# Sums inside DRAM placed over heads 0 to 3 instead of in one block, four of them listed for the page stage; sample values, index scales and index keys reordered

## The chip, the cores and the metric

The kernel runs on one core of a Trainium2 chip. Its engines are the matrix engine (PE, whose weight loads are shown as PEld), the vector engine (DVE), the scalar engine (ACT), GpSimd (POOL) and the sync engine (SP), which here only issues DMAs; POOL issues some too. Each engine works through its own queue of instructions in the order in which the program gives them, and waits on semaphores. The metric is the device time of one execution in microseconds (us), lower is better; the number given is the median of several executions.

## The reference

One inference step of a single decoder layer with two groups of heads: sparse indexer attention (8 heads of 128) and gated linear attention (4 heads, keys of 128, values of 256). There are 512 prompt tokens and 64 sample tokens (8 sequences of 8), which attend to 1024 cached positions held in pages of 128. Everything is float32, the model width is 2048.

```python
h = RMSNorm(x)                                  # prompt and sample rows alike
z = einsum('btd,de->bte', h, w_in)              # one projection for all groups
qa, ka, va, ga, qi, ki, wi, qb, kb, vb, gb, ab = split(z)
# sparse attention: score every position by the indexer, keep the best 256 (128 in the prompt), attend to those
dots = einsum('bthd,bsd->btsh', qi, ki) * D_IDX ** -0.5
sc   = einsum('btsh,bth->bts', relu(dots), wi)  # causal, then top_k
p    = softmax(q . k_selected * DH_A ** -0.5);  o = p . v_selected
# gated linear attention: S <- diag(a_t) S + k_t v_t ; o_t = q_t S  (chunked)
y = RMSNorm(x + concat(silu(ga) * o_A, silu(gb) * o_B) @ w_out)
```

It returns y, the new keys, values and index keys, and the new recurrent states.

## The kernel before

**Weights.** Each 128x512 block of weights comes through `wload`: a DMA from SP into `w_raw` (three buffers), a cast on ACT to the rounded half `w_hi` (L196, five buffers), and the rest `w_lo = w_raw - w_hi` (L199, five buffers), which POOL makes in heads 0 to 3 and DVE elsewhere (`lo_eng`). PE multiplies xh by w_hi, xl by w_hi and xh by w_lo (L251 in columns of 288, L256, and L664 to L666 in columns of 512), so each product has nearly float32's precision. `wloads` and `rounded` hold the DMAs and casts so far, and `issue_after` puts an instruction behind one of them.

**Heads.** `head(h)` projects q, k, v and g for one attention head, scores it (L736 to L738, `pq` from `kh`, `kl` and `qh`, `ql`; `kh` is the cast of the rotated keys, L632), and writes the gated result to DRAM. Head 0 is followed by `vgroup(0)`, which makes the values of heads 0 to 3. Into the heads a background is woven: first the indexer's scores for the sample pages (`sample_scores`, index keys `kc` from pages, split into `kch` and `kcl`, L505 to L517), then the top-k rounds (MAX8 and MATCH_REPLACE on DVE), and from head 4 on the *page stage*, `units`: it loads pages of cached keys and values (`kt`, `vt`) and scores them (`pS`, L283 to L286), one beat of a generator for each weight block.

**Sums of output weights.** The output projection uses sums of blocks of `w_out`. `block_parts` yields 16 parts of 512 KB into the DRAM tensor `spill_t[1]` (`st` in the profile): each is a copy from DRAM to DRAM, issued by SP, and then an accumulating DMA issued by POOL. Parts 0 to 7 add further blocks of `w_out`; parts 8 to 11 add the finished parts 0 to 3, and parts 12 to 15 the finished parts 8 to 11. Other sums (`spill_t[0]`) are made by `block_sums` in the page stage, eight of them. Before, the list `started` issues one copy with each weight load after `vgroup(0)` (16 in a row, L194), and the list `added` one add behind each of POOL's w_lo from head 2 on (16 in a row, L203).

**Scales.** `squares` and what follows make `rstd`, the norm's factor for each token, by matmuls with diagonal matrices (`ps_st`, L405). It scales the index keys (`kiT`, `ab`, L409 to L414) and twice the index weights of the sample (`wiT`, called `sS` in the profile, L416), which a matmul `pU` (L418) spreads.

**Recurrence.** `recur` runs a head of gated linear attention over four prompt blocks: state update `pUg`, output `pO` (L1232), state `Sst` (L1241), then the sample part, which needs the sample's values `vs` as halves (`vSg` loaded from DRAM, cast at L1220, subtracted at L1221).

**What sets the order.** The program is written in Python order, but a scheduler with a timeline of its own orders the instructions of each engine; `high_priority` and `issue_after` steer it. So the order built can differ from the text.

Of the kernel before, what the change touches and what calls it, by code (L numbers as in the profile page):

```python
# [20 lines left out]
P = 128  # L21
# [98 lines left out]
def build(tc, I, O):  # L120
# [61 lines left out]
        return t[:, 32:544] if far else t[:, :512]  # L182

    SUMS = ((0, 0), (0, 1), (1, 1), (1, 0))
    started, added = [], []

    def wload(src, far=0):
        with tc.high_priority(offset=WOFF):
            raw = wp.tile([P, 512], F32, name="w_raw", tag="w_raw", bufs=3)
            d = sy.dma_start(raw, src)  # L190
            wloads.append(d.ins if hasattr(d, "ins") else d)
            if started:
                with tc.issue_after(wloads[-1]):
                    sy.dma_start(*started.pop(0))  # L194
            hi = wp.tile([P, 512], F32R, name="w_hi", tag="w_hi", bufs=5)
            c = se.copy(hi, raw)  # L196
            rounded.append(getattr(c, "ins", c))
            lo = low_tile(wp, 5, far)
            c = lo_eng[0].tensor_tensor(out=lo, in0=raw, in1=hi.bitcast(F32), op=ALU.subtract)  # L199
            if lo_eng[0] is po_:  # L200
                if added:
                    with tc.issue_after(getattr(c, "ins", c)):
                        po_.dma_start(*added.pop(0), accum_op=ALU.add)  # L203
        return hi, lo

    first_w = {}
# [188 lines left out]
    def token_scales():  # L395
        se.activation(sst, sst, AF.Sqrt, bias=eps, scale=1.0 / D)
        ve.reciprocal(out=sst, in_=sst)
        ve.tensor_tensor(out=sst2, in0=sst, in1=sst, op=ALU.mult)
        for j in range(2):
            pst = mm1("ps_st")  # L400
            for i in (range(4), (4,))[j]:
                n = (P, TS)[j]
                dg = pr.tile([P, P], F32, name="dg", bufs=2)
                ve.tensor_scalar(out=dg[:, :n], in0=ident[:, P - n :], scalar1=sst[:, i : i + 1], scalar2=None, op0=ALU.mult)
                pe.matmul(pst[:, P * (i % 4) : P * (i % 4) + n], ones, dg[:, :n], start=True, stop=True)  # L405
            c = (slice(0, TP), slice(TP, T))[j]
            se.copy(rstd[:, c], pst[:, : c.stop - c.start])

        ve.tensor_mul(kiT, kiT, rstd[0:64])  # L409
        sy.dma_start(O["kiT"], kiT)  # L410
        ab = keys[:, :T]
        ve.tensor_tensor(out=v2(ab[64:96]), in0=ps0[64:96], in1=v2(rstd[64:96]), op=ALU.mult)
        se.copy(abS[64:96], ab[64:96])
        ve.tensor_tensor(out=abS[96:128], in0=ab[64:96], in1=abS[64:96].bitcast(F32), op=ALU.subtract)  # L414
        for _ in range(2):
            ve.tensor_tensor(out=wiT[:, TP:T], in0=wiT[:, TP:T], in1=rstd[0:16, TP:T], op=ALU.mult)  # L416
        pu = mm1("pU")
        pe.matmul(pu[:, :TS], e16[0:16], wiT[:, TP:T], start=True, stop=True)  # L418
        for half in range(2):
            for e in range(2):  # L420
                c = 16 * half + DT * e
                ve.tensor_tensor(
                    out=wall[:, half].rearrange("p (m e) c -> p m e c", e=2)[:, :, e, c : c + DT],
                    in0=pu[:, :TS].rearrange("p (m e t) -> p m e t", e=2, t=DT)[:, :, e, :],
                    in1=dt8.unsqueeze(1).to_broadcast([P, 4, DT]), op=ALU.mult,
                )
# [52 lines left out]
    def sample_scores():  # L479
# [14 lines left out]
        for half in range(2):  # L494
            for grp in range(2):
                for m in range(4):
                    if half and m == grp == 0:
                        weigh(0)
                    b = 2 * m + grp
                    hr, other = ((slice(0, 64), slice(64, 128)), (slice(64, 128), slice(0, 64)))[m % 2]  # L500
                    if m % 2 == 0:
                        kc = pa.tile([P, 512], F32, name="kc", bufs=2)
                    raw = kc[hr]
                    page_dma(lambda j: raw[:, P * j : P * (j + 1)], lambda r: I["cidx"][r].rearrange("o d s -> (o d) s"), b * NPAGE + 4 * half, 4)
                    kch = pa.tile([P, 512], F32R, name="kch", tag="kch", bufs=2)  # L505
                    se.copy(kch[hr], raw)
                    po_.tensor_copy(kch[other], raw)
                    kcl = pa.tile([P, 512], F32R, name="kcl", bufs=2)
                    with tc.high_priority(offset=WOFF // 2):
                        ve.tensor_tensor(out=kcl[hr], in0=raw, in1=kch[hr].bitcast(F32), op=ALU.subtract)  # L510
                        se.copy(kcl[other], kcl[hr].bitcast(F32))
                    yield
                    pq = mm1("pq")
                    pe.matmul(pq, lq[b], kch, start=True, stop=False)
                    pe.matmul(pq, lq[b], kcl, start=False, stop=True)
                    rl = pa.tile([P, 512], F32, name="rl", bufs=8)
                    se.activation(rl, pq, AF.Relu)  # L517
                    rls.append(rl)
# [132 lines left out]
    def vgroup(g, step):  # L651
# [46 lines left out]
            if g < 2:  # L698
                sy.dma_start(O["v"][r, cols], vt)
        if g == 0:  # L700
            po_.memset(vaS[:TS], 0.0)
        to = vaS[TS:, cols] if g < 2 else ev.tile([P, 512], F32, name="v_smp", tag="e1", bufs=2)[TS:]
        se.copy(to, accs[4][:TS])
        ve.tensor_tensor(out=to, in0=accs[4][TS:], in1=to, op=ALU.add)
# [77 lines left out]
    def head(h, bg, n):  # L782
        if h == 1:
            q, k = qk1
        else:
            q = head_q(h)
            pump(bg, n)
            k = head_k(h)
            pump(bg, n)
        if h == 0:  # L790
            for f in (head_q, head_k):
                qk1.append(f(1))
                pump(bg, n)
            vgroup(0, lambda k: pump(bg, 2) if k % 4 == 3 else None)
            filler[0] = None
            for _ in first:
                pass
            pa_s.close()
            px["p"], px["s"] = pool("pd1", 1)
            pump(bg, 3)  # L800
            for to, src, _ in block_parts():
                started.append((to, src))
        if h == 2:
            assert not started
            for to, _, more in block_parts():
                added.append((to, more))
        Pi = head_scores(h, q, k)
        if h == 4:
            vgroup(1, lambda k: None)
        v = head_v(h)  # L810
        g1 = head_g(h)
        pump(bg, min(n, 4))
        head_out(h, Pi, v, g1)

    qk1 = []


    mixS = gaS
# [1 line left out]
    def units(un, hg, pages):  # L820
        later, count = [], [0, 0]

        def block_sums():
            n = count[1]
            count[1] += 1
            t = un.tile([P, 4, 512], F32, name="bs", tag="kv", bufs=pages)
            for j, (half, q) in enumerate(SUMS):
                sy.dma_start(t[:, j, :], I["wo"][q, :, 8 * half + n, :])

            def add():  # L830
                ve.tensor_tensor(out=t[:, 0:2, :], in0=t[:, 0:2, :], in1=t[:, 1:3, :], op=ALU.add)
                ve.tensor_tensor(out=t[:, 2, :], in0=t[:, 2, :], in1=t[:, 0, :], op=ALU.add)
                ve.tensor_tensor(out=t[:, 3, :], in0=t[:, 3, :], in1=t[:, 2, :], op=ALU.add)

            later.append((count[0] + 2, add))
            later.append((count[0] + 3, lambda: sy.dma_start(spill_t[0][:, :, n, :], t)))

# [22 lines left out]

        for _ in unit_steps(un, hg, fetch, rest):
            count[0] += 1
            while later and later[0][0] <= count[0]:
                later.pop(0)[1]()
            yield
        for _, f in later:
            f()
# [1 line left out]
    def unit_steps(un, hg, fetch, rest):  # L869
        kv = fetch(0, 0, 0)  # L870
        yield
        if hg == 0:
            yield from rest(2)
        for w in range(2):
            qz = ev.tile([P, 4, 4, 32], F32, name="qz", tag="e0", bufs=2)
            po_.memset(qz, 0.0)
# [100 lines left out]
    head(2, bg, 4)  # L977
    head(3, bg, 4)
    lo_eng[0] = ve
    assert not added  # L980
    with tc.issue_after(px["end"]):
        for _ in bg:
            pass
# [225 lines left out]
    def recur(h, eL, qE, kDt, ks):  # L1209
        vtok = gl.tile([P, 4, DV], F32, name="vtok")  # L1210
        sv = spill_v[2 + h // 2][:, DV * (h % 2) : DV * (h % 2) + DV]
        with tc.issue_after(wloads[-1]):
            sy.dma_start(vS[:TS], sv[TP:])
            sy.dma_start(vtok, sv[:TP].rearrange("(i p) c -> p i c", p=P))
        vs = [gl.tile([96, DV], F32R, name=f"vs{w}") for w in range(2)]
        for w in range(2):
            r = slice(32 * w, 32 * w + 32)
            with tc.issue_after(rounded[-1]):
                for r0 in (0, 32):
                    se.copy(vs[w][r0 : r0 + 32], vS[r])  # L1220
            ve.tensor_tensor(out=vs[w][64:96], in0=vS[r], in1=vs[w][r].bitcast(F32), op=ALU.subtract)  # L1221


        osb = gl.tile([P, 5, DV], F32, name="osb")
        ss = gl.tile([P, 5], F32, name="ss", bufs=2)
        S = None
        for i in range(4):
# [11 lines left out]
            with ahead():  # L1239
                if S is None:  # L1240
                    ve.tensor_copy(Sn, pU[:, :DV])  # L1241
                else:
                    ve.scalar_tensor_tensor(out=Sn, in0=S, scalar=eL[:, i : i + 1], in1=pU[:, :DV], op0=ALU.mult, op1=ALU.add)
            S = Sn
        sy.dma_start(O["sp"][h], S)

        pO = mm1("pO")
# [425 lines left out]
```

## Time and profile before

| | us |
|---|---|
| median of 3 executions | 1194.14 (1193.59 to 1195.24) |
| the profiled execution | 1196.54 |
| its span in the trace | 1194.8 |
| PE busy | 1180.8 |
| DVE / ACT / POOL busy | 727.3 / 585.2 / 311.7 |
| DMA moved | 259.98 MB, mean 218 GB/s |

The profiled execution lies 2.40 us above the median, and 1.74 us of its time lie outside the span. PE is the engine to watch: the others have idle time everywhere. PE's matmuls overlap, so a busy time per matmul can't be added up; waits of PE are where time can be won. Below, start times are counted from the start of the span, DMA times go from issue to landing, and a wait is put down to what ended it.

### The profile page before, as it was taken

To read this page: it belongs to the slowest core of one execution; us is meant where nothing else is said; L and a number is where in the kernel's file an instruction comes from. 1 tells how busy PE (TensorE), PEld (TensorE's weight loads), DVE (VectorE), ACT (ScalarE), POOL (GpSimd) and SP (SyncE) were. 2 spreads that over 40 slices of the span, in tenths; PEclk is the share of its full clock that TensorE was granted. 3 is DMA by queue.
4 is the path that set the end of the run, shared out by engine and by line. 5 is a ranking of instruction groups with operands and counts; after the bars stand their busy time and mean duration, and the time that the engine had idled before them with its cause. 6 is when DMAs were issued, how large, how long until landed. Compare 5 with 4: busy or idle time off the path is not lost.

```text
span 1194.8 us, 22991 instructions
## 1 busy us (share of the span) xinstructions
PE 1180.8 (99%) x8389; PEld 1040.1 (87%) x8389; DVE 727.3 (61%) x1347; ACT 585.2 (49%) x1045; POOL 311.7 (26%) x495
## 2 busy tenths in 40 slices
PE   9999999999999999999999999999999999999997
PEld 8999987899989778899988769778899999888886
DVE  7678899799646433575445424434556444657786
ACT  6887564444443232354344435336367533544454
POOL 1225665536621110200213311321042211012100
PEclk9999999999999999999999999999999999999999
DMA  8552233777973999998857675667715377669873
GB/s 298 204 171 102 91 106 108 267 242 165 223 179 91 365 315 359 339 321 307 287 198 267 221 258 204 220 226 246 258 50 178 123 253 233 228 169 238 249 229 119
DMA packets 142419, 259.98 MB, mean 218 GB/s; under 512 B 15633, under 2 KB 38818, under 8 KB 141730
## 3 DMA queue, kind: packets, MB, share of 16 engines
q1 hardware_dynamic: 136370, 243.83, 60.7%
q0 software_dynamic: 4928, 13.11, 6.4%
q10 hardware_dynamic: 1008, 1.57, 0.4%
q8 instruction: 66, 1.08, 0.4%
q14 instruction: 47, 0.39, 0.1%
HBM read 224.62 MB, written 50.48 MB: 230 GB/s over the span
## 4 chain that ended last, share of the span: by engine, by line
PE 90%; DMA 4%; DVE 3%; issue 1%; SPq 1%; ACT 1%; POOL 0%; DVEq 0%; ACTq 0%; POOLq 0%
PE ps_g L251 37%; PE ps_g L256 6%; PE ps_g L664 5%; PE ps_g L666 5%; PE ps_g L665 5%; PE acc L1392 4%; PE acc L1393 4%; PE acc L1394 4%; DMA w_raw<-in_w 2%; PE pS L286 2%; PE pOs L286 2%; PE acc_s L1398 1%; PE acc_s L1397 1%; PE ps_v L660 1%; PE ps_v L661 1%
## 5 line engine op out<-in xcount | busy, mean ns | idle before, releaser
L251 PE MATMUL ps_g<-xh,w_hi 128*128 128x288 f32 x1312 | 391.6, 298 | 0.0
L251 PE MATMUL ps_g<-xl,w_hi 128*128 128x288 f32 x1312 | 287.9, 297 | 0.0
L251 PE MATMUL ps_g<-xh,w_lo 128*128 128x288 f32 x1312 | 283.9, 295 | 0.4 <-DVE w_lo L219 0.2
L196 ACT CAST w_hi<-w_raw 128x512 fp32r<-128x512 f32 x252 | 154.0, 619 | 261.8 <-PE ps_g L251 82.5
L251 PEld LDWEIGHTS ps_g<-xh,w_hi 128*128 128x128 f32 x1312 | 246.3, 188 | 3.6 <-issue 1.7
L199 DVE TENSOR_TENSOR w_lo<-w_raw,w_hi 128x512 fp32r<-128x512 f32 x188 | 132.6, 712 | 183.5 <-ACT w_hi L196 174.9
L251 PEld LDWEIGHTS ps_g<-xl,w_hi 128*128 128x128 f32 x1312 | 212.1, 188 | 2.3 <-issue 1.2
L251 PEld LDWEIGHTS ps_g<-xh,w_lo 128*128 128x128 f32 x1312 | 211.2, 188 | 1.8 <-DVE w_lo L219 0.5
L199 POOL TENSOR_TENSOR w_lo<-w_raw,w_hi 128x512 fp32r<-128x512 f32 x64 | 87.6, 1370 | 55.2 <-ACT w_hi L196 46.8
L664 PE MATMUL ps_g<-w_hi,xh 128*128 128x512 f32 x256 | 100.9, 396 | 0.0
L666 PE MATMUL ps_g<-w_hi,xl 128*128 128x512 f32 x256 | 100.3, 392 | 0.0
L665 PE MATMUL ps_g<-w_lo,xh 128*128 128x512 f32 x256 | 100.1, 391 | 0.0
L1387 DVE TENSOR_TENSOR w_lo<-w_raw,w_hi 128x1024 fp32r<-128x1024 f32 (+1 forms) x60 | 68.4, 1150 | 40.1 <-ACT w_hi L1385 39.7
L1385 ACT CAST w_hi<-w_raw 128x1024 fp32r<-128x1024 f32 (+1 forms) x60 | 59.6, 994 | 64.6 <-PE acc_s L1397 27.2
L1393 PE MATMUL acc<-w_lo,fh 128*128 128x512 f32 x216 | 84.0, 389 | 0.0
L1394 PE MATMUL acc<-w_hi,fl 128*128 128x512 f32 x216 | 84.0, 389 | 0.0
L1392 PE MATMUL acc<-w_hi,fh 128*128 128x512 f32 x216 | 83.5, 389 | 0.0
L666 PEld LDWEIGHTS ps_g<-w_hi,xl 128*128 128x128 f32 x256 | 48.1, 188 | 10.7 <-issue 0.8
L664 PEld LDWEIGHTS ps_g<-w_hi,xh 128*128 128x128 f32 x256 | 48.0, 188 | 10.0 <-DVE ev_t L624 0.3
L665 PEld LDWEIGHTS ps_g<-w_lo,xh 128*128 128x128 f32 x256 | 48.1, 188 | 9.7
L1394 PEld LDWEIGHTS acc<-w_hi,fl 128*128 128x128 f32 x216 | 40.5, 188 | 8.5
L1392 PEld LDWEIGHTS acc<-w_hi,fh 128*128 128x128 f32 x216 | 40.6, 188 | 8.4
(396 smaller groups left out, 2085.2 us busy)
## 6 DMA issues: line engine op xcount, KB each, us to landing
w_raw<-in_w SPq DMA_DIRECT2D x188, 256.0 KB, 4.0
kt<-in_ck SPq DMA_DIRECT2D x128, 256.0 KB, 5.1
vt<-in_cv SPq DMA_DIRECT2D x128, 256.0 KB, 5.3
w_raw<-in_wv SPq DMA_DIRECT2D x64, 256.0 KB, 3.4
w_raw<-st SPq DMA_DIRECT2D x32, 512.0 KB, 4.8
w_raw<-in_wo SPq DMA_DIRECT2D x20, 512.0 KB, 5.5
st<-in_wo SPq DMA_DIRECT2D x16, 512.0 KB, 4.9
bs<-in_wo SPq DMA_DIRECT2D x32, 256.0 KB, 5.4
```

The lines of the kernel that those rows point to most:

```text
L196: c = se.copy(hi, raw)
L199: c = lo_eng[0].tensor_tensor(out=lo, in0=raw, in1=hi.bitcast(F32), op=ALU.subtract)
L251: pe.matmul(ps[:, j, :HT], wt, xt[k][:, j * HT : (j + 1) * HT], start=(k == 0 and n in (0, 2)), stop=(k == NK - 1 and n > 3))
L256: m = pe.matmul(ps[:, 0, :TQ], wt[:, c], xt[:, P:T], start=(k == 0 and n == 0), stop=(k == NK - 1 and n == 2))
L664: pe.matmul(accs[i], xh[k][:, c], wh, start=a, stop=False)
L665: pe.matmul(accs[i], xh[k][:, c], wl, start=False, stop=False)
L666: m = pe.matmul(accs[i], xl[k][:, c], wh, start=False, stop=b)
L1385: se.copy(hi, raw)
L1387: ve.tensor_tensor(out=lo, in0=raw, in1=hi.bitcast(F32), op=ALU.subtract)
L1392: pe.matmul(acc, f[0][:, k, c], wh, start=a, stop=False)
L1393: pe.matmul(acc, f[0][:, k, c], wl, start=False, stop=False)
L1394: return pe.matmul(acc, f[1][:, k, c], wh, start=False, stop=b)
```

## The change

1. Copies and adds of the DRAM sums go by a table, `moves`: after `vgroup(0)` the weight loads are counted in slots; the copy of part n goes with slot 2n and its add with slot 2n + 6, for parts 0 to 11. Parts 12 to 15 go to a list `late`, out of which `block_sums` takes them in the page stage.
2. The two products of the sample's index weights with `rstd` stand ahead of those of the index keys.
3. The index key pages `kc` have three buffers instead of two.
4. The page stage rests three beats instead of two at its start; its list `later` may hold entries out of order.
5. The memset of `vaS` on POOL is put behind the last w_lo.
6. In `recur` the split of the sample's values stands behind the second block instead of ahead of the first.

```diff
+    moves, slot = ({}, {}), [None]
+
+    def move(side, lead):
+        for f in moves[side].pop(slot[0], ()):
+            with tc.issue_after(lead):
+                f()
...
             wloads.append(d.ins if hasattr(d, "ins") else d)
-            if started:
-                with tc.issue_after(wloads[-1]):
-                    sy.dma_start(*started.pop(0))
+            move(0, wloads[-1])
...
-            if lo_eng[0] is po_:
-                if added:
-                    with tc.issue_after(getattr(c, "ins", c)):
-                        po_.dma_start(*added.pop(0), accum_op=ALU.add)
+            lows.append(getattr(c, "ins", c))
+            move(1, lows[-1])
+            if slot[0] is not None:
+                slot[0] += 1
...
+        for _ in range(2):
+            ve.tensor_tensor(out=wiT[:, TP:T], in0=wiT[:, TP:T], in1=rstd[0:16, TP:T], op=ALU.mult)
         ve.tensor_mul(kiT, kiT, rstd[0:64])
...
-        for _ in range(2):
-            ve.tensor_tensor(out=wiT[:, TP:T], in0=wiT[:, TP:T], in1=rstd[0:16, TP:T], op=ALU.mult)
...
-                        kc = pa.tile([P, 512], F32, name="kc", bufs=2)
+                        kc = pa.tile([P, 512], F32, name="kc", bufs=3)
...
-            po_.memset(vaS[:TS], 0.0)
+            with tc.issue_after(lows[-1]):
+                po_.memset(vaS[:TS], 0.0)
...
-            for to, src, _ in block_parts():
-                started.append((to, src))
-        if h == 2:
-            assert not started
-            for to, _, more in block_parts():
-                added.append((to, more))
+            parts = list(block_parts())
+            for n, (to, src, more) in enumerate(parts[:12]):
+                moves[0][2 * n] = [partial(sy.dma_start, to, src)]
+                moves[1][2 * n + 6] = [partial(po_.dma_start, to, more, accum_op=ALU.add)]
+            late.extend(parts[12:])
+            slot[0] = 0
...
+            if n >= 4:
+                to, src, more = late.pop(0)
+                later.append((count[0] + 1, lambda: sy.dma_start(to, src)))
+                later.append((count[0] + 4, lambda: po_.dma_start(to, more, accum_op=ALU.add)))
             later.append((count[0] + 2, add))
...
-            while later and later[0][0] <= count[0]:
-                later.pop(0)[1]()
+            for f in [x for x in later if x[0] <= count[0]]:
+                later.remove(f)
+                f[1]()
...
-            yield from rest(2)
+            yield from rest(3)
...
-        vs = [gl.tile([96, DV], F32R, name=f"vs{w}") for w in range(2)]
...
             S = Sn
+            if i == 1:
+                vs = [gl.tile([96, DV], F32R, name=f"vs{w}") for w in range(2)]
...
```

In the built order of the new file, lines are numbered higher than before: L199 is L204, L460 is L465, L1064 is L1076, L1241 is L1244, and the moved L1221 is L1255. L843 is the copy of a late part and L844 its add; L190 of the new file is a DMA that `move` issues.

POOL at the end of head 2 and in head 3, where the adds of parts 8 to 15 go (`st1`); `w_lo` 4156 (4158 before) is the weight of slot 22. Before:

```order
193 L203 DMA st1_560<-in_wo 128x1024
195 L199 TENSOR_TENSOR w_lo_4245<-w_raw_4241,w_hi_4243 128x512 [waits DMAHW5_49,Activation_49]
196 L203 DMA st1_560<-st1_560 128x1024 [waits DMASW0_49]
197 L199 TENSOR_TENSOR w_lo_4276<-w_raw_4272,w_hi_4274 128x512 [waits DMAHW6_49,Activation_49]
198 L203 DMA st1_560<-st1_560 128x1024 [waits DMASW1_49]
200 L199 TENSOR_TENSOR w_lo_4307<-w_raw_4303,w_hi_4305 128x512 [waits DMAHW7_49,Activation_49]
201 L203 DMA st1_560<-st1_560 128x1024 [waits DMASW2_49]
202 L199 TENSOR_TENSOR w_lo_4338<-w_raw_4334,w_hi_4336 128x512 [waits DMAHW4_49,Activation_49]
203 L203 DMA st1_560<-st1_560 128x1024 [waits DMASW3_49]
204 L199 TENSOR_TENSOR w_lo_4449<-w_raw_4445,w_hi_4447 128x512 [waits DMAHW0_49,Activation_49]
205 L203 DMA st1_560<-st1_560 128x1024 [waits DMASW4_49,DMASW0_49]
```

Now:

```order
191 L204 TENSOR_TENSOR w_lo_4156<-w_raw_4151,w_hi_4154 128x512 [waits DMAHW0_49,Activation_49]
192 L190 DMA st1_560<-st1_560 128x1024 [waits DMASW0_49]
194 L204 TENSOR_TENSOR w_lo_4187<-w_raw_4183,w_hi_4185 128x512 [waits DMAHW2_49,Activation_49]
195 L844 DMA st1_560<-st1_560 128x1024 [waits DMASW1_49,DMASW0_49]
197 L204 TENSOR_TENSOR w_lo_4242<-w_raw_4238,w_hi_4240 128x512 [waits DMAHW5_49,Activation_49]
198 L190 DMA st1_560<-st1_560 128x1024 [waits DMASW2_49]
199 L204 TENSOR_TENSOR w_lo_4273<-w_raw_4269,w_hi_4271 128x512 [waits DMAHW6_49,Activation_49]
201 L844 DMA st1_560<-st1_560 128x1024 [waits DMASW3_49,DMASW2_49]
202 L204 TENSOR_TENSOR w_lo_4303<-w_raw_4299,w_hi_4301 128x512 [waits DMAHW7_49,Activation_49]
203 L190 DMA st1_560<-st1_560 128x1024 [waits DMASW4_49]
205 L844 DMA st1_560<-st1_560 128x1024 [waits DMASW5_49,DMASW4_49]
211 L844 DMA st1_560<-st1_560 128x1024 [waits DMASW7_49,DMASW6_49]
```

The adds of parts 12 to 15 have moved not to the page stage but between those of parts 8 to 11, and each waits for the add issued one weight earlier, where before it waited for one issued four weights earlier.

SP at the very start, where it loads the first full blocks of weights. Before:

```order
40 L190 DMA w_raw_462<-in_w 128x512 [waits DMAHW1_49,DVE_49]
41 L190 DMA w_raw_480<-in_w 128x512 [waits DMAHW2_49,DVE_49]
42 L460 DMA ptab_524<-in_page_table 1x128 [waits DMAHW3_49]
45 L190 DMA w_raw_708<-in_w 128x512 [waits DMAHW6_49,DVE_49]
47 L190 DMA w_raw_726<-in_w 128x512 [waits DMAHW1_49,DMAHW0_49,DVE_49]
```

Now:

```order
40 L197 DMA w_raw_462<-in_w 128x512 [waits DMAHW1_49,DVE_49]
41 L843 DMA st1_560<-in_wo 128x1024 [waits DMAHW2_49]
42 L843 DMA st1_560<-in_wo 128x1024 [waits DMAHW3_49]
43 L843 DMA st1_560<-in_wo 128x1024 [waits DMAHW4_49]
44 L197 DMA w_raw_480<-in_w 128x512 [waits DMAHW5_49,DVE_49]
48 L197 DMA w_raw_708<-in_w 128x512 [waits DMAHW1_49,DVE_49]
50 L843 DMA st1_560<-in_wo 128x1024 [waits DMAHW3_49]
51 L197 DMA w_raw_726<-in_w 128x512 [waits DMAHW4_49,DVE_49]
```

The copies of the four late parts have moved to the start of the program, three of them ahead of one weight load and one ahead of a later one.

DVE in the first recurrence, the split of the sample's values (`vs0`, `vs1`) and the first state. Before:

```order
827 L199 TENSOR_TENSOR w_lo_9468<-w_raw_9464,w_hi_9466 128x512 [waits DMAHW6_49,Activation_49]
828 L1221 TENSOR_TENSOR vs0_9172<-vSg_7805,vs0_9172 32x256 [waits DMAHW3_49,Activation_49]
829 L1221 TENSOR_TENSOR vs1_9173<-vSg_7805,vs1_9173 32x256 [waits Activation_49]
830 L1064 SCALAR_TENSOR_TENSOR qT_9167<-ps_g_9026,rstd_596 128x576 [waits PE_49]
831 L1241 COPY Sst_9189<-pUg_9182 128x256 [waits PE_49]
```

Now:

```order
827 L204 TENSOR_TENSOR w_lo_9468<-w_raw_9464,w_hi_9466 128x512 [waits DMAHW6_49,Activation_49]
828 L1255 TENSOR_TENSOR vs0_9193<-vSg_7805,vs0_9193 32x256 [waits DMAHW3_49,Activation_49]
829 L1255 TENSOR_TENSOR vs1_9194<-vSg_7805,vs1_9194 32x256 [waits Activation_49]
830 L1076 SCALAR_TENSOR_TENSOR qT_9167<-ps_g_9026,rstd_596 128x576 [waits PE_49]
831 L1244 COPY Sst_9181<-pUg_9174 128x256 [waits PE_49]
```

Nothing has moved here: the two subtractions still stand ahead of the state.

More of the change, by code (lines that the diff above doesn't have):

```diff
@@ L184, in build @@
     SUMS = ((0, 0), (0, 1), (1, 1), (1, 0))
-    started, added = [], []
+    moves, slot = ({}, {}), [None]
[3 more added lines that the diff above has]
+                f()
+    lows = []
     def wload(src, far=0):
@@ L813, in head @@
         head_out(h, Pi, v, g1)
-    qk1 = []
+    qk1, late = [], []
     mixS = gaS
@@ L979, in build @@
     lo_eng[0] = ve
-    assert not added
+    slot[0] = None
+    assert not any(moves)
     with tc.issue_after(px["end"]):
@@ L1214, in recur @@
             sy.dma_start(vtok, sv[:TP].rearrange("(i p) c -> p i c", p=P))
-        vs = [gl.tile([96, DV], F32R, name=f"vs{w}") for w in range(2)]
[L1216 to L1221, printed above, removed]
         osb = gl.tile([P, 5, DV], F32, name="osb")
@@ L1244, in recur @@
             S = Sn
+            if i == 1:
+                vs = [gl.tile([96, DV], F32R, name=f"vs{w}") for w in range(2)]
+                for w in range(2):
+                    r = slice(32 * w, 32 * w + 32)
+                    with tc.issue_after(rounded[-1]):
+                        for r0 in (0, 32):
+                            se.copy(vs[w][r0 : r0 + 32], vS[r])
+                    ve.tensor_tensor(out=vs[w][64:96], in0=vS[r], in1=vs[w][r].bitcast(F32), op=ALU.subtract)
         sy.dma_start(O["sp"][h], S)
```

## The prediction

> **What bounds the kernel now.** I read the page first, then the waits of the matrix engine (PE), then the stretch of the DRAM sums by DMA queue, by chain and by timeline.
>
> ```profile
> span 1194.8 us, 22991 instructions
> PE 1180.8 (99%) x8389; PEld 1040.1 (87%) x8389; DVE 727.3 (61%) x1347; ACT 585.2 (49%) x1045; POOL 311.7 (26%) x495
> PEclk9999999999999999999999999999999999999999
> ```
>
> PE is busy 99% of the span, at the full clock. The change removes no matmul, so it can win only time in which PE stands still. The view of waits (us in total, times, longest) lists where:
>
> ```profile
> PE pq L736 <- ACT kh L632: 2.8, 1, 2.8
> ...
> PE pO L1232 <- DVE Sst L1241: 0.9, 1, 0.9
> PE pq L515 <- ACT kcl L511: 0.7, 1, 0.7
> PE pS L283 <- issue: 0.5, 1, 0.5
> PE pU L418 <- ACT w_hi L196: 0.4, 1, 0.4
> ```
>
> Left out is a filler matmul's wait at the kernel's start. These are five single stalls: 2.8 + 0.9 + 0.7 + 0.5 + 0.4 = 5.3 us, or 0.44% of the span. That is the most that the change can win. What it can lose has no such ceiling. From no change this kernel's measurement can tell about 0.2%, 2.4 us, so the forecast is made stall by stall.
>
> **The 2.8 us stall: head 3's first score matmul.** First from the DMA queues of 280 to 350 us and the chain of 300 to 350 us (start, length, what), then the weight loads' row in section 6 of the page, and the landing times of the adds: of all 16, of the one issued at 313.4, of the one at 315.3.
>
> ```profile
> q0 software_dynamic: 2304, 8.39, 67.6%
> ...
> 333.75 0.67 POOL st L203
> ...
> 334.49 1.56 POOL w_lo L199
> ...
> 336.07 9.90 DMA w_raw<-in_w
> ...
> 346.07 0.62 ACT w_hi L196
> 346.69 0.53 ACT kh L632
> ...
> 347.26 0.33 PE pq L736
> ```
>
> ```profile
> w_raw<-in_w SPq DMA_DIRECT2D x188, 256.0 KB, 4.0
> ...
> DMA to landing us min/median/max: 6.2/8.3/11.2
> ...
> DMA to landing us min/median/max: 6.2/6.2/6.2
> ...
> DMA to landing us min/median/max: 8.5/8.5/8.5
> ```
>
> The adds, issued by POOL, keep all 16 DMA engines busy for 67.6% of 70 us: 47.3 us, 2.96 us for each of 16. A weight load takes 4.0 us to land in the run's median; the one that matters took 9.9. It waited for a buffer that POOL's w_lo of 334.49 freed; behind it come w_hi, then kh on the same engine, then PE at 347.26, 2.8 us late, so that PE was ready at about 344.5.
>
> The change spreads twelve of the sums: copies from slot 0 on, adds from slot 6 on, one per two weights. Eight adds (j = 0 and 1) are then done where weights are made well ahead of use, and I cost these and the twelve copies at nothing: no wait of L251 on one of POOL's w_lo is in the list above. If that cover were gone, such waits would appear. But the last four sums don't go to the page stage in the built order. POOL's rows show each of their adds (L844 of the new file) in between the weights of slots 23 to 29, behind a wait for DMASW0, 2, 4 or 6: the landing of the add issued one weight earlier, whose result it reads. POOL runs in order, so w_lo of the next weight waits with it. The chain per pair: add, landing L, issue of L844 (0.67, as L203 in the chain), w_lo 1.28, next add. The first of the four leaves at 302.86:
>
> ```profile
> 301.63 1.28 POOL L199 TENSOR_TENSOR w_lo<-w_raw,w_hi 128x512 fp32r<-128x512 f32 x1 [0.39 <-ACT w_hi L196]
> 302.86 0.81 POOL L203 DMA_DIRECT2D st<-in_wo  x1
> ```
>
> Four landings and four times 1.9 us (0.67 + 1.28) later, the w_lo that frees the buffer is done: 302.9 + 4L + 7.6 = 310.5 + 4L, against 336.05 before. Then comes the weight load. With no backlog I take 5 us, nearer to the median of 4.0 than to 9.9. w_hi and kh add 1.2. kh is ready at 316.7 + 4L:
>
> - L = 6.2 (the add of 313.4, the least of the sixteen): 341.5, no stall, 2.8 us won.
> - L = 8.3 (the median): 349.9, a stall of 5.4, 2.6 us lost.
> - 7.6: kh at 347.1, nothing won or lost.
>
> Which L? In each pair but the first, the add follows an L844 by 1.9 us, which is what the add of 315.3 did after that of 313.4; it took 8.5, with a third one on its heels, which the new order doesn't have: I take 7.9. The first add is as alone as that of 313.4: 6.2. Together 6.2 + 3 x 7.9 = 29.9, kh at 346.6 instead of 347.2: **0.6 us won**, between 2.8 won and 3.4 lost (all four at 8.5).
>
> **The 0.9 us stall: the recurrence.** The source moves the split of the sample values (vs) behind the second block. In the built order ACT's casts, DVE's two subtractions and SP's load stand where they stood, ahead of Sst:
>
> ```profile
> 728.51 1.67 ACT L1220 CAST vs<-vSg 32x256 fp32r<-32x256 f32 x4 [3.78 <-DMA vSg<-sv]
> ...
> 730.21 0.42 DVE L1221 TENSOR_TENSOR vs<-vSg,vs 32x256 fp32r<-32x256 f32 x1 [0.85 <-ACT vs L1220]
> ...
> 731.34 0.41 DVE L1241 COPY Sst<-pUg 128x256 f32<-128x256 f32 x1
> ```
>
> The load (vSg) lands at 728.5, the casts and the subtractions follow, and Sst waits behind them on DVE. Nothing of that is different: **0**, with 0.9 won as the far end, if the load came earlier.
>
> **The 0.5 us stall: the page stage.** PE waited for the last page (kt) of its first scores.
>
> ```profile
> 400.50 0.39 PE L660 MATMUL ps_v<-w_hi,xs 128*128 128x512 f32 x1
> 400.73 0.39 PE L661 MATMUL ps_v<-w_lo,xs 128*128 128x512 f32 x1
> 401.57 0.59 PE L283 MATMUL pS<-kt,qz 128*32 128x512 f32 x1 [0.45 <-issue]
> ```
>
> One more beat of rest puts two more matmuls, 0.23 us apart by their starts, ahead of the scores: **0.4 won**, 0 to 0.5. The page loads are SP's and stand in the same order, so nothing new is late.
>
> **The 0.7 us stall: index keys.**
>
> ```profile
> 169.92 1.27 DVE L510 TENSOR_TENSOR kcl<-kc,kch 64x512 fp32r<-64x512 f32 x1
> 171.22 0.62 ACT L511 CAST kcl<-kcl 64x512 fp32r<-64x512 f32 x1 [0.81 <-DVE kcl L510]
> ```
>
> DVE made kcl late, and ACT's cast waited for it, so a third buffer for the keys is no remedy by itself. DVE's order now has one round of the top-k fewer ahead of it, but its work behind rstd starts later. **0.3 won**, between 0.7 won and 0.7 lost.
>
> **The 0.4 us stall: index scales (pU).**
>
> ```profile
> 131.00 2.87 DVE L416 TENSOR_TENSOR sS<-sS,rstd 16x64 f32<-16x64 f32 x1
> 131.14 1.28 POOL L199 TENSOR_TENSOR w_lo<-w_raw,w_hi 128x512 fp32r<-128x512 f32 x1
> 132.38 1.42 POOL L613 TENSOR_TENSOR c_s<-c_s,rstd 128x576 f32<-128x576 f32 x1
> 133.98 0.40 PE L418 MATMUL pU<-sS,c_e 16*128 16x64 f32 x2 [0.44 <-ACT w_hi L196]
> ...
> L416 DVE TENSOR_TENSOR sS<-sS,rstd x2: 214/1544/2874, 130.2 to 131.0; 16x64 f32<-16x64 f32 x2
> ```
>
> Two equal products of 16x64 took 0.21 and 2.87 us; the long one ended with two POOL instructions that ran beside it. The products now come before the key products, but PE's last sum before rstd stands about 21 matmuls later, and pU only 12. The one nearly cancels the other: **0.1 lost**, between 0.4 won and 2.7 lost (the second product held like the first). The Trainium skill, "SBUF — State Buffer", section "Who interferes with whom", says that a DVE instruction with two SBUF inputs and a GpSimd one that reads SBUF take their shared port by an exclusive lock, for the whole instruction. The rows agree (2.87 against 0.21). By that rule both products can be held, since POOL has three such instructions in a row there, and the sum below would be 2.6 us higher.
>
> **What the hoisted copies cost.** Three of the four "late" copies now stand on SP between two weight loads at 24 us, the fourth three loads on.
>
> ```profile
> q1 hardware_dynamic: 7907, 16.74, 73.4%
> st<-in_wo SPq DMA_DIRECT2D x16, 512.0 KB, 4.9
> ```
>
> ```profile
> 24.01 0.82 SPq L190 DMA_DIRECT2D w_raw<-in_w  x2
> 28.84 1.35 DVE L199 TENSOR_TENSOR w_lo<-w_raw,w_hi 128x512 fp32r<-128x512 f32 x2 [2.33 <-ACT w_hi L196]
> 39.48 1.33 DVE L199 TENSOR_TENSOR w_lo<-w_raw,w_hi 128x512 fp32r<-128x512 f32 x2
> 44.03 0.36 PE L256 MATMUL ps_g<-xh,w_lo 128*128 128x448 f32 x1
> ```
>
> From 200 to 270 us queue q1 moved 16.74 MB in 73.4% of 70 us, 3.07 us per MB, so a copy of 0.52 MB is 1.6 us (my estimate by bytes), three are 4.8. The second weight of 24.01 comes that much later; the tightest weight behind it, the first of 39.48, is made by 40.2 and used at 44.03, 3.9 in hand. If the whole delay reaches it, PE waits 0.9; if ACT's idle time takes some of it, less: **0.6 lost**, from 0, and up to 3 x 4.9 - 3.9 = 10.8 if the copies passed one at a time at their landing time, which I think far off, since sixteen of them went through that stretch beside weights. A rule speaks against the change here: the Trainium skill, "DMA: Bandwidth & Descriptors", section "Two DMAs through the same engine are not ordered", has descriptors within one queue of an engine start in order, so the weight can't pass the copies. By it the loss is up to 0.9; if it could pass them, 0, and the sum 0.6 lower.
>
> **The rest.** Scheduler-made reorderings between 380 and 700 us may open new small waits; nearest are those of 0.4 and 0.5 above: **0.3 lost**, 0 to 0.9. vaS's memset and the out-of-order list hide under work that POOL and the sequencers have free.
>
> **Sum.** -0.6 + 0 - 0.4 - 0.3 + 0.1 + 0.6 + 0.3 = -0.3 us. The profiled execution took 1196.54 (1.74 more than its span), 2.40 above the median of the runs, 1194.14; against itself that gives 1196.2, against the median 1193.8. The largest gain asked for, 2.8, is given back in POOL's new waits.
>
> **Rivals.**
> - *The adds land alone, L = 6.2 to 6.8.* Then kh is ready by 343.9, head 3's stall is gone: -2.8 in place of -0.6, sum -2.5, 1191.6; with pU's or kcl's stall gone as well, 1190.9. For it: the one st<-st add that found no backlog; against it: the pairs on each other's heels.
> - *POOL's waits decide (slower).* At L = 8.3 head 3 waits 5.4: +2.6 in place of -0.6, sum +2.9, 1197.0. For it: the median landing; against: that median comes from a backlog. It decides from L = 7.6 on.
> - *Port or copies (slower).* Both scale products held, or the copies slower than their bytes say: +2.6, 1196.4 to 1197.
>
> **How the numbers follow.** Forecast 0.45, within 0.2%; first rival 0.30, faster; second 0.18 and third 0.07, slower. The range takes the first rival's far end, 1190.6, and reaches past the second's to 1197.2; outside lie L above 8.4 and copies far dearer, 0.2 together. The forecast's own range is 1192 to 1196.3.
>
> **What would show it.** Right: the wait of pq on kh in head 3 is 1.5 to 3 us; POOL's w_lo from 305 to 340 us show idle time before them that ends with an add's landing; the pO wait is still 0.9; a wait of 0.3 to 1 near 44 us. Wrong: no wait at that pq (first rival), or one above 4.5 (second); adds at L844 landing outside 7 to 8.5; L844 issued after 400 us.

## Result and profile after

The changed kernel took 1208.66 us in the median (1206.80 to 1208.79, four runs), the kernel before 1193.87 (1192.92 to 1195.24, four runs): a ratio of 1.0109, 95% interval 1.0089 to 1.013. It is slower by 1.1%, where no change was forecast and 1197.2 was the upper end. (The two medians by themselves are 1.24% apart, inside that interval.) The profiled execution is the fastest of the four, 1206.80; its span is 1205.0, which is 10.2 us above the span of before. The medians lie 14.8 us apart, so what follows accounts for the two traced executions, and not for all of the difference of the medians.

Parts 1 and 2 of the page of the changed kernel (busy time, share, instructions; PE clock in 40 slices):

```profile
span 1205.0 us, 22969 instructions
PE 1186.4 (98%) x8389; PEld 1044.9 (87%) x8389; DVE 731.0 (61%) x1347; ACT 586.0 (49%) x1045; POOL 310.4 (26%) x495
PEclk9999999999989999999999999999999999999999
```

PE issues the same 8389 matmuls, and yet is busy 5.6 us longer (1186.4 against 1180.8): some of them ran slower. The PE clock shows an 8 in the slice from 331 to 362 us. Its waits (us in total, times, longest):

```profile
PE pq L742 <- ACT kh L637: 4.2, 1, 4.2
PE pq L520 <- ACT kcl L516: 2.3, 1, 2.3
...
PE pt L766 <- DVE p L755: 1.0, 3, 0.5
PE ps_g L256 <- POOL w_lo L204: 0.9, 1, 0.9
PE pq L744 <- DVE kl L638: 0.7, 1, 0.7
PE ps_g L261 <- DVE w_lo L204: 0.7, 1, 0.7
PE pS L288 <- issue: 0.4, 1, 0.4
PE pO L1235 <- DVE Sst L1244: 0.3, 1, 0.3
```

Two waits have grown, head 3's kh from 2.8 to 4.2 and the index keys' kcl from 0.7 (at 172 us) to 2.3 (at 153 us), and four places are new. Only pU's wait is gone, and pO's and pS's are smaller. Where the 10.2 us lie can be worked out from the start times of PE's n-th matmul in the two traces, since both have equally many (inside a stretch the n-th need not be the same matmul, as the built orders differ):

| stretch (time before, us) | lost there, us |
|---|---|
| to 142 (0.7 lost near 44, pU's 0.4 won) | +0.2 |
| 142 to 153 (wait on kcl) | +4.5 |
| 153 to 179 (kcl's old wait, now gone) | -1.2 |
| 179 to 325 (heads 1 to 3; three small waits make 1.5 of it) | +2.7 |
| 325 to 360 (0.9 for a w_lo, then head 3's wait on kh, and after) | +5.1 |
| the rest | -1.1 |

At both large places more is lost than the wait grew by. The view of windows shows why (us, PE busy and instructions, PEld, DVE, ACT, POOL, then PE's granted clock, DMA share, GB/s):

```profile
148.00:152.00 4.00, 2.61 (x20) 2.34 (x18) 3.97 (x8) 0.74 (x2) 2.82 (x3) 1.00 0.08 25
152.00:156.00 4.00, 3.07 (x14) 3.03 (x15) 3.94 (x11) 2.99 (x6) 1.21 (x3) 0.69 0.12 33
156.00:160.00 4.00, 4.00 (x27) 3.85 (x27) 3.90 (x10) 2.79 (x7) 1.72 (x3) 0.89 0.54 165
352.00:356.00 4.00, 0.00 (x0) 0.00 (x0) 3.44 (x4) 1.17 (x3) 1.18 (x2) 0.86 0.85 263
356.00:360.00 4.00, 3.98 (x16) 3.98 (x17) 3.32 (x9) 0.49 (x1) 0.00 (x0) 0.50 0.56 195
360.00:364.00 4.00, 4.00 (x24) 3.88 (x23) 1.09 (x5) 1.97 (x3) 0.00 (x0) 0.79 0.00 0
```

After each of the two waits the granted clock falls to half for some microseconds (in windows of half a microsecond it is 0.50 from 153.5 to 156.5 and from 356 to 361.5), and PE, though busy, gets through 16 matmuls in 4 us where it else does some 30. By the four rows in which PE worked below full clock, that took 4 x (0.31 + 0.11 + 0.50 + 0.21) = 4.5 of the 5.6 us (my estimate). In the kernel before, 2.8 us of waiting at 344 left the clock at 1.00. So in this trace an idle PE cost the wait and then a slower restart.

The chain of waits in head 3 of the changed kernel (start, length, what):

```profile
307.34 1.23 POOL w_lo L204
308.58 6.48 DMA st<-st
...
320.94 5.20 DMA far<-turned
326.21 0.61 POOL st L844
...
328.01 8.84 DMA st<-st
...
337.24 0.29 POOL st L844
...
343.74 4.45 issue
...
348.78 1.58 POOL w_lo L204
350.38 4.36 DMA w_raw<-in_w
354.83 0.62 ACT w_hi L201
355.45 0.53 ACT kh L637
356.02 0.47 PE pq L742
```

This is the chain that the prediction laid out, add, landing, L844, w_lo, weight load, w_hi, kh, with POOL standing still between. In two of its four links the view names something else: a load of the top-k (far) at 320.94 and "issue" at 343.74. The landing times of the adds issued at 318.9 and 339.1 settle both:

```profile
DMA to landing us min/median/max: 6.9/6.9/6.9
...
DMA to landing us min/median/max: 8.8/8.8/8.8
```

They landed at 325.8 and 347.8, and each of the four L844 begins 0.4 us behind the landing of the add ahead of it. In the built order the L844 of 326.21 waits for POOL's own DMAs alone, so the far load that landed at 326.1 is not what held it. POOL's timeline (start, length, what, and in brackets its idle time ahead and what ended that); the adds moved with the weights are at L190, the late adds, each of which reads the result of the one ahead, at L844:

```profile
308.58 0.83 POOL L190 DMA_DIRECT2D st<-st  x1
...
315.46 0.82 POOL L844 DMA_DIRECT2D st<-st  x1 [2.62 <-DMA st<-st]
...
318.88 0.80 POOL L190 DMA_DIRECT2D st<-st  x1
...
326.21 0.83 POOL L844 DMA_DIRECT2D st<-st  x1 [3.17 <-DMA far<-turned]
...
328.01 1.12 POOL L190 DMA_DIRECT2D st<-st  x1
...
337.24 0.81 POOL L844 DMA_DIRECT2D st<-st  x1 [6.79 <-DMA st<-st]
...
339.05 1.08 POOL L190 DMA_DIRECT2D st<-st  x1
...
348.21 0.85 POOL L844 DMA_DIRECT2D st<-st  x1 [4.47 <-DMA st<-st]
```

POOL, which makes the weights here, waits 2.6, 3.2, 6.8 and 4.5 us for these landings.

### The profile page after: what moved, and what is told of

Same layout as the page of the kernel before. It is cut to its first block, busy times and chain, and to the rows that moved or that the text cites. A ratio compares the mean times of both kernels' runs of the same rounds, so it can differ in the third digit from the quotient of the medians.

```text
span 1205.0 us, 22969 instructions
## 1 busy us (share of the span) xinstructions
PE 1186.4 (98%) x8389; PEld 1044.9 (87%) x8389; DVE 731.0 (61%) x1347; ACT 586.0 (49%) x1045; POOL 310.4 (26%) x495
## 4 chain that ended last, share of the span: by engine, by line
PE 83%; DMA 8%; DVE 4%; issue 2%; ACT 1%; POOL 1%; SPq 1%; POOLq 0%; DVEq 0%; ACTq 0%
PE ps_g L256 33%; PE ps_g L669 5%; PE ps_g L670 5%; PE ps_g L671 5%; PE ps_g L261 4%; PE acc L1405 4%; PE acc L1403 4%; PE acc L1404 4%; PE pOs L291 2%; PE pS L291 2%; DMA st<-st 1%; DMA xr<-in_xT 1%; PE acc_s L1409 1%; PE acc_s L1408 1%; PE ps_v L665 1%
## 5 line engine op out<-in xcount | busy, mean ns | idle before, releaser
L204 DVE TENSOR_TENSOR w_lo<-w_raw,w_hi 128x512 fp32r<-128x512 f32 x188 | 136.7, 734 | 168.6 <-ACT w_hi L201 165.1
L204 POOL TENSOR_TENSOR w_lo<-w_raw,w_hi 128x512 fp32r<-128x512 f32 x64 | 86.9, 1364 | 43.5 <-ACT w_hi L201 33.5
L1396 ACT CAST w_hi<-w_raw 128x1024 fp32r<-128x1024 f32 (+1 forms) x60 | 59.6, 995 | 65.2 <-PE acc_s L1408 24.4
L680 POOL CAST xs<-xh 128x64 fp32r<-128x64 f32 x64 | 21.6, 338 | 104.2 <-PE ps_v L666 99.0
L630 POOL TENSOR_TENSOR ev_sw<-ev_sw,c_s 128x576 f32<-128x576 f32 x16 | 25.2, 1572 | 88.6 <-ACT ev_sw L627 88.5
```

## Experiments

Theory A after the result: all of the loss comes from the four late sums, which the scheduler hoisted, in two separate places. Their copies at the start bring the loss near 150 us; their adds between POOL's w_lo bring the loss in head 3. Rival B put the loss near 150 us down to the other parts of the change. The first four runs are a square: late copies early or not, late adds between weights or not, and the sums as before. Ratios are against the kernel before on the same chip, so they are compared rather than the times.

**Late sums really in the page stage** (`e1`):

```diff
-                later.append((count[0] + 1, lambda: sy.dma_start(to, src)))
-                later.append((count[0] + 4, lambda: po_.dma_start(to, more, accum_op=ALU.add)))
+                later.append((count[0] + 1, lambda: pin(lambda: sy.dma_start(to, src))))
+                later.append((count[0] + 4, lambda: pin(lambda: po_.dma_start(to, more, accum_op=ALU.add))))
+    def pin(f):
+        with tc.issue_after(wloads[-1]):
+            f()
```

> The change as its words say: the four late copies are held behind the last weight load, so that they and their adds really stand in the page stage (copies on SP and adds on POOL from head 4 on); all else as in the changed kernel. Theory A (all of the loss comes from the four late sums being hoisted: their copies to the start, their adds between POOL's w_lo): 1191 to 1194.5 us, no wait of pq on kh above 1.5 us in head 3, no stall near 150 us, granted clock 1.00 at 150 to 160 and 350 to 365. Rival B (the stall near 150 us comes from the third key buffer, the order of the scales or the memset, and stays): 1196 to 1199, with the wait of pq on kcl still over 2 us. Rival C (the twelve spread sums themselves crowd the DMA engines): head 3 still waits over 2.5 us for kh.

Measured: 1198.25 us against 1195.15, ratio 1.0022 (1.0011 to 1.0033). The time misses theory A's range and lies in rival B's. The profiled execution is the fastest of the ten, 1195.69, with a span of 1193.8, below that of before, so its trace can't show what the median has lost. Its waits:

```profile
PE pq L520 <- ACT kcl L516: 1.2, 2, 1.0
PE ps_v L665 <- POOL xs L681: 1.1, 1, 1.1
```

Head 3's wait on kh is gone, the wait near 150 us is down to 1.0, and the clock stays at 1.00 in both places. So the waits that rivals B and C need aren't there, though the 1.0 near 150 is a small part of B that holds: it is there in every run that has all the other parts of the change and no early copies (e1, e3, e4, e6, e8), while before, e7 and e9, without them, wait 0.7 at 171. Four fifths of the loss go with the hoisting. The rest of 0.2% was not expected; small waits at 276 to 317 us (pt 0.8, pq on kl 0.7) and one of 1.1 us at 662 remain, and what makes it up is open. It goes with the place of the sums: e4 below, with the sums as before and all else as here, is 0.28% faster than e1 on the same chip.

**Only the copies early** (`e2`; the adds behind POOL's last w_lo):

```diff
-                later.append((count[0] + 4, lambda: po_.dma_start(to, more, accum_op=ALU.add)))
+                later.append((count[0] + 4, lambda: pin(lambda: po_.dma_start(to, more, accum_op=ALU.add))))
+    def pin(f):
+        with tc.issue_after(last_po[0]):
+            f()
```

> The late copies stay hoisted to the start of the program, their adds are held behind POOL's last w_lo, so nothing of POOL's weights waits for them. Theory A, with two separate places: the early half of the loss alone, 1197 to 1200 us: about 0.8 us near 44 and about 4.5 us near 150 (a stall of 2.3 us and the slower clock behind it), nothing in head 3 beyond 1 us. Rival B gives the same here. If the two places depend on one another (the adds wait because everything is 4 us later), more than 1203.

Measured: 1199.82 us, ratio 1.0032 (1.0017 to 1.0048). The waits of the early half are there, and head 3 waits 1.0:

```profile
PE pq L520 <- ACT kcl L516: 2.3, 1, 2.3
...
PE pq L742 <- ACT kh L637: 1.0, 1, 1.0
...
PE ps_g L261 <- DVE w_lo L204: 0.7, 1, 0.7
```

But here the clock did not fall behind the wait of 2.3 us, against what was expected, as its windows show:

```profile
152.00:156.00 4.00, 2.81 (x19) 2.67 (x20) 3.97 (x9) 2.74 (x5) 0.95 (x3) 1.00 0.10 27
156.00:160.00 4.00, 4.00 (x31) 3.91 (x30) 3.87 (x10) 3.01 (x6) 2.10 (x2) 1.00 0.56 168
```

**Only the adds between weights** (`e3`; the copies in slots 1, 3, 5, 7):

```diff
-                later.append((count[0] + 1, lambda: sy.dma_start(to, src)))
+            for n, (to, src, _) in enumerate(late):
+                moves[0][2 * n + 1] = [partial(sy.dma_start, to, src)]
```

> The late copies go out with weight slots 1, 3, 5 and 7, so nothing stands at the start; their adds stay between POOL's w_lo of head 3, each behind the landing of the add before. Theory A: the late half of the loss alone, 1199 to 1202 us: waits at 280 to 330 us together about 2.5 us, pq on kh 3 to 4.5 us and a slower clock behind it, nothing near 150. Rival B: 1203 to 1206, since the stall near 150 is then still there.

Measured: 1206.20 us, ratio 1.0081 (1.0051 to 1.0111): the larger part of the loss, and 4 us above the upper end of what theory A gave; by the time alone it is nearer to rival B's 1203 to 1206. Its waits:

```profile
PE pq L742 <- ACT kh L637: 4.5, 1, 4.5
...
PE pq L520 <- ACT kcl L516: 1.2, 2, 1.0
```

And its windows behind that wait (columns as above):

```profile
352.00:356.00 4.00, 2.69 (x11) 2.69 (x12) 2.55 (x6) 1.66 (x3) 0.24 (x1) 0.61 0.57 209
356.00:360.00 4.00, 4.00 (x19) 4.00 (x19) 1.69 (x8) 0.62 (x2) 0.00 (x0) 0.53 0.15 53
```

Nothing waits at 150 us beyond 1.0, so the wait that rival B needs is not there. The square, in excess over 1: neither half 0.22% (e1), copies early 0.32%, adds between weights 0.81%, both 1.09%. Above e1 the halves are 0.10% and 0.59%, both together 0.87%. The intervals are 0.1 to 0.3% to either side, and e2's overlaps e1's, so the times don't tell whether the halves simply add. That the two places are separate rests on the waits: e2 has 2.3 us near 150 and 1.0 in head 3, e3 1.0 and 4.5.

**The sums as before, the rest of the change kept** (`e4`): the `started` and `added` lists of before in place of `moves` and `late`.

> The sums as in the kernel before (16 copies, then 16 adds in head 2 and 3), all other parts of the change kept: scales first, three key buffers, memset behind the weights, page stage one beat later, sample values later in the text. Theory A: 1193 to 1195 us, head 3's wait 2.8 us as before, pU's wait gone or 0.4. Rival B: 1196 to 1199, with a stall near 150 us.

Measured: 1194.92 us, ratio 0.9994 (0.9984 to 1.0004). The other five parts together make no difference: pU's wait is gone, kcl's is 1.0 instead of 0.7. Head 3 waits 0.8 for kh and 0.6 for a later score, where 2.8 was expected, since the adds stand as before; why it is less is open.

**Tables first** (`e5`): how do copies at 24 us make kcl late at 150? One path was SP's order, since the rotation tables (c_c, c_s) were issued 4 us later, behind weight 39.

```diff
-            d = sy.dma_start(raw, src)
+            with tc.issue_after(tables[-1]) if len(wloads) == 39 else ExitStack():
+                d = sy.dma_start(raw, src)
```

> The changed kernel with one order set by hand: the load of weight 39 waits on SP until the rotation tables (c_c, c_s) are issued, as they stood before; the late copies stay at the start and the late adds between POOL's w_lo. Theory A1 (near 150 us the early copies cost through SP's order: the tables are issued 4 us later, behind a weight load that waits for POOL, and DVE's queue stands behind the rotation): the wait of pq on kcl falls from 2.3 to 1.0 us or less, the clock stays at 1.00 from 150 to 160, 1203.5 to 1205.5 us. Rival A2 (the copies are late for the norm's factors, rstd itself, whatever the order of SP): the wait stays at 2 us or more, 1207 to 1209.

Measured: 1207.05 us, ratio 1.0089 (1.0062 to 1.0116), and kcl's wait is still 2.2, though the tables were issued at 126.8 and 127.2 us, within 0.6 us of before. So A1 falls: the tables alone don't make the wait. What is late in both is rstd. The second of its two copies on ACT (start, length), by the timeline of the kernel before:

```profile
128.38 0.21 ACT L407 COPY rstd<-ps_st 128x64 f32<-128x64 f32 x1
```

by that of the changed kernel:

```profile
130.82 0.20 ACT L412 COPY rstd<-ps_st 128x64 f32<-128x64 f32 x1
```

and by that of e1:

```profile
127.99 0.21 ACT L412 COPY rstd<-ps_st 128x64 f32<-128x64 f32 x1
```

In the changed kernel it is 2.4 us later than before and 2.8 later than in e1, and in the built order the matmul ahead of it is PE's number 702 instead of 683, in the changed kernel and in e2 and e5, but not in e1. The first kcl behind it, on DVE, starts at 151.54 us instead of e1's 145.79, and that is 5.8 us: the delay grew on the way. In the changed kernel DVE stood 1.3 us for POOL's ev_sw, which stands behind the late table c_s; its product sS took 1.30 us instead of 0.21, two products for sc (L480) 1.72 instead of 0.89, and one more ev_t stands ahead of kcl.

**The same copies, ten weights on** (`e8`; as e2, but `issue_after(wloads[10])` around the copies): the same copies, issued at 41.7 to 43.8 us instead of 24.4 to 30.9 in the changed kernel, and PE's order near 120 us as without them (683).

> As the run with the late copies early only, but the four copies are held behind the eleventh weight load of 512 columns (some 45 to 55 us) instead of standing at the start. They are as many, as early with respect to head 0, and their adds still stand behind POOL's last w_lo; the built order of PE near 120 to 150 us is again that without hoisted copies (the last matmul for rstd is number 683, not 702). Theory A3 (the early copies cost by what they do to the order that the scheduler builds and by the one weight near 44 us): no wait near 44, pq on kcl 1.0 to 1.2 us, 1195.5 to 1198 us and 2 us or more below the copies at the start. Rival (the copies' traffic ahead of head 0 costs wherever it stands): pq on kcl 2 us or more, 1199 to 1201.

Measured: 1196.61 us, ratio 1.0004 (0.999 to 1.0018), against e2's 1.0032, which differs in the copies' place alone (but ran on another chip). kcl's wait is 1.0, none is left near 44. So it isn't the copies' bytes that cost there, but their place: at the very start they make one weight late, and with them there the scheduler builds another order, in which rstd comes later. That the later rstd alone makes the wait on kcl was not tried by itself; a wait of over 2 us and the late rstd go together in every run here.

**All sixteen by slots, none late** (`e6`): copy n at slot 7n/4, add at 7n/4 + 5, so that an add is seven slots from the one that it reads. The traffic of adds is the same, and POOL has nothing to wait for.

```diff
-            for n, (to, src, more) in enumerate(parts[:12]):
-                moves[0][2 * n] = [partial(sy.dma_start, to, src)]
-                moves[1][2 * n + 6] = [partial(po_.dma_start, to, more, accum_op=ALU.add)]
-            late.extend(parts[12:])
+            for n, (to, src, more) in enumerate(parts):
+                moves[0][7 * n // 4] = [partial(sy.dma_start, to, src)]
+                moves[1][7 * n // 4 + 5] = [partial(po_.dma_start, to, more, accum_op=ALU.add)]
```

> The changed kernel with no late list: all 16 parts by slots, copy n at slot 7n/4 and add n at slot 7n/4 + 5, so that an add comes seven slots (some 25 us) behind the one whose result it reads, and POOL needs not wait for a landing. Theory A (the wait for the landing holds POOL, not the adds' traffic): kh's wait of head 3 below 1.5 us, no slower clock, 1192 to 1196 us. Rival D (the traffic of adds in head 3 delays the weights by itself): kh's wait 2.5 us or more, 1197 to 1202.

Measured: 1193.86 us, ratio 0.9984 (0.9961 to 1.0006). No wait on kh in head 3 at all, though the adds still take long; the DMA issues from 300 to 350 us, first in the changed kernel, then here:

```profile
st<-st POOLq DMA_DIRECT2D x8, 512.0 KB, 6.2
```

```profile
st<-st POOLq DMA_DIRECT2D x6, 512.0 KB, 8.3
```

8.3 us to landing in the median, longer than the changed kernel's 6.2. In head 3 it is the waiting on POOL that costs, not the adds: rival D falls.

**The same on the kernel before, alone** (`e7`, and `e9` with more executions):

> The same placing of all 16 sums by slots, on the kernel before: scales, key buffers, memset, page stage and sample values as before. If the placing is what helps and the other parts are neutral (as with the sums as before): within 0.15% of e6, 1191 to 1196 us. If the other parts carry a gain of their own: 2 us or more above e6.

Measured: 1193.66 us, ratio 0.9978 (0.9955 to 1.0000).

> The same kernel as the run with all 16 in slots on the kernel before, with more rounds. If its gain is real: 0.997 to 0.999 of the kernel before, with an interval that excludes 1. If it was noise: 0.9995 to 1.001.

Measured: 1193.60 against 1196.52, ratio 0.9975 (0.996 to 0.999). This beats the kernel before by 0.25%, with an interval that excludes 1: head 3's wait is gone and nothing has come in its place. Its waits:

```profile
PE pq L520 <- ACT kcl L516: 0.7, 1, 0.7
PE pO L1236 <- DVE Sst L1245: 0.5, 1, 0.5
PE pU L423 <- ACT w_hi L201: 0.4, 1, 0.4
```

**And the scales first** (`e10`: e9 with the change's second part):

> All 16 in slots, and of the other parts the scales ahead of the index keys alone. The wait of pU (0.4 us) goes; if DVE's work ahead of kcl is as before, kcl's wait stays 0.7 and the time is 0.4 us below the run without the scales; if the scales put kcl off, its wait is 1.0 and the time the same within 0.3 us. Either way 0.996 to 0.999 of the kernel before.

Measured: 1193.82 us, ratio 0.9977 (0.9964 to 0.999). pU's wait is gone, kcl's has grown to 1.4; no gain beyond e9.

## Why the prediction was wrong

- **The late sums are hoisted.** Right, from the built order, and e1 shows that four fifths of the loss go with it. Of the two large places the prediction saw head 3; the one near 150 us stood in its sum as a gain.
- **kcl, -0.3, and pU, +0.1: the step that failed first.** The prediction saw PE's last matmul for rstd stand "about 21 matmuls later", weighed it against pU alone, and noted for kcl only that "its work behind rstd starts later". The delay went through DVE's queue to kcl and grew from 2.8 to 5.8 us on the way: 2.3 us of wait instead of 0.4, at an earlier place, with the clock's drop behind it. By the table that place lost 3.3 us in all (4.5 less 1.2). For pU the cost was taken too high: its wait is gone, so 0.4 was won.
- **Head 3's term, -0.6: wrong in sign.** The mechanism, POOL standing for each landing, was right. The wait of 4.2 lies outside the 1.5 to 3 that would have shown the prediction right and short of the 4.5 of the second rival, to which it is nearest. From the first of the four adds to the end of kh the chain took 47.4 us (308.58 to 355.98), where the sum had 43.7 (302.9 to 346.6). The landings L were 6.5, 6.9, 8.8 and 8.8, together 31.0 against 29.9. Each L844 began 0.4 us behind its landing, 1.6 in all, which the sum left out. The four stretches from an L844 to the next add (the last to the end of its w_lo) made 9.2 instead of 7.6, in part since POOL waited 1.0 for a w_hi in the first. The weight load, 4.4 instead of 5, gave 0.6 back, and PE came 1.6 us later to this place, counted from the first add. So L alone was not far off; taking 7.9 for the last pairs was still a guess, and they took 8.8. The sign "adds at L844 landing outside 7 to 8.5" came true (5.6 to 5.9), but those are not the adds that POOL waited for.
- **The slower clock: missing.** The sum had only waits. Of PE's 5.6 us of extra busy time some 4.5 go with the clock, by the estimate above; e1 and e2, at full clock in both places, are busy 0.8 and 1.3 longer than before too. The prediction's price of a rival, 5.4 us of wait in head 3, had no term for what follows a wait. Waits of 4.2, 4.5 and 4.6 us (the changed kernel, e3, e5) were each followed by windows at 0.50 to 0.61. Of four waits of 2.2 to 2.8 us one was followed by 0.69 (the changed kernel) and three by 1.00 (before, e2, e5): in these rows no such length decides by itself. The Trainium skill, "TensorE: Matmul & The Clock Gate", section "What's actually happening", says that after an idle window of about 3.4 us the clock is halved, and that the window runs freely. The waits above 4 us agree. A drop after 2.3 us is earlier than the page's figure, and here the measurement counts; that the same wait ends in either way would fit a window that runs freely, which no run here shows by itself.
- **Early copies, +0.6: right.** 0.7 us, the wait of L261 on DVE's w_lo, near 44 us; and none in e8.
- **Recurrence, 0.** ACT's, DVE's and SP's orders stayed as read. The wait was 0.3 instead of 0.9, as it is 0.2 to 0.6 in some other runs whose order there is the same: it follows when its load lands, and the 0.6 won is luck (the first cast on it began 1.1 us behind PE's first state update before, 0.5 now).
- **Page stage, -0.4:** 0.4 left of 0.5, so 0.1 was won. **The rest, +0.3:** too small, and in another place: pt, kl and w_lo wait 2.4 us between 280 and 351 us, none of them in e6. The 0.9 of it on a w_lo of POOL comes at 350 us, behind the last of the late adds; the prediction looked for such a wait at the spread sums alone.

## What to carry to other kernels

Where a scheduler sets the order, look where the moved instructions land, and then cost the queue behind each of them up to the next thing that the bottleneck waits for, not only the first reader. A DMA that must wait for another one's landing doesn't belong in the queue of an engine that feeds the bottleneck: put enough work between the two, as e6 and e9 do with seven weights instead of one. And where the profile has granted clocks, look at them behind each long wait of the matrix engine: here a wait above 4 us cost some 3 us more at half clock, and one of 2 to 3 us cost more in one trace of four.

## What the runs showed of the hardware that was not expected

- After PE stood still for 4.2 to 4.6 us (the changed kernel, e3, e5), its granted clock was 0.50 to 0.61 in the next 4 us in which it worked; after 2.2 or 2.3 us it was 0.69 in one trace and 1.00 in two others; after 2.8 us 1.00.
- The time to land of an accumulating DMA of 512 KB from DRAM to DRAM went with its distance from the one ahead. Of those that POOL then waited for in the changed kernel, e3 and e5, the six issued 1.8 us behind another landed in 8.4 to 9.6 us, the three issued 2.1 to 3.4 us behind in 6.9 to 7.4, and the three issued 7.2 us behind in 6.5 to 8.0.
- POOL's dependent add began 0.4 us behind the landing that it waited for, each of the four times in the changed kernel.
